# The SSM groups of a hybrid encoder layer as a table of steps: one core of a Trainium2 chip

## The chip, the core and the metric

The kernel runs on one core of one Trainium2 chip. The metric is the time of one execution in microseconds (us) as the device counts it; three runs of the kernel before were taken. The profile is one more execution, with the hardware profiler on; its rows count from the first instruction (the span).

Engines: PE is TensorE's matmul, PEld its weight load, DVE VectorE, ACT ScalarE, POOL GpSimd, SP the engine whose queue issues most DMAs. Each engine works through its own instructions in the order in which the program gives them.

## What is computed

One layer of a bidirectional encoder on 4096 tokens of width 1024, float32:

```
h = RMSNorm_pre(x)
[ssm_u | ssm_gate | pool_u | pool_gate | q | k | v | attn_gate] = h @ W_in
y_ssm  = GLU(GELU(bidirectional S5 complex-diagonal SSM(ssm_u) + D*ssm_u)) * silu(ssm_gate)
y_pool = scale * GroupLinear(centred multi-scale mean pool(pool_u) - pool_u) * silu(pool_gate)
y_attn = windowed GQA(+-128 tokens, ALiBi, sink)(q, k, v) * silu(attn_gate)
x = x + RMSNorm_post(concat(y_ssm, y_pool, y_attn) @ W_out)
```

The SSM has 16 groups of 16 channels, 64 complex states in each of two directions. A state follows h_t = lambda * h_(t-1) + B u_t with a complex lambda; y = Re(C h), summed over both directions, + D u.

## The kernel before, in words

**Stages.** TensorE multiplies float32 operands as pairs of a rounded high part and the rest (`split`, L187: ScalarE copies the high part, another engine subtracts it to get the low part, `lo_part`, one slot later), three matmuls for each product (`mm3`, L977). Pass 1 (8 blocks of 512 tokens) projects the pooling and SSM inputs, pass 2 q, k, v with the attention beside it, pass 3 the gates of SSM and attention, with the sixteen SSM groups beside it. Then comes the product with W_out, with the GLU, the pooling and the norm beside it.

**Slots.** Order is written out by hand. `Slots` (L84) holds a list of what to issue in each slot; `step()` closes one. In the projection passes a slot is 6 matmuls: a chunk (128 output channels x 512 tokens) has 24, so four slots; a block of pass 3 has six chunks, 24 slots. Chunks alternate between PSUM banks 0 and 1; a chunk's result `mm` is taken out by ScalarE in the slot after its end (`ev_g`, L1092: Silu to `gg`, stored three slots later as `sgate` or `agate`). What the program issues in a slot is added to each engine's queue; nothing else ties engines to slots, so they run ahead or behind as far as semaphores let them. `e.at` puts a function in a slot, `e.gen` a generator, whose `yield n` waits n slots. `settle` issues all that is left under a label.

**SSM groups.** `to_p3` (L1353) runs in slot 422 (block 17 of 24, its slot 14). It opens the tiles (`p3_open`, L954), where the GLU's weights are loaded and split at once (L971 to L974), and starts one generator `ssm_group` (L982) for each group, 8 slots apart (`SSM_PACE`). The sequence of eight tokens is folded into the channel dimension (128 rows = 8 tokens x 16 channels), which leaves 512 steps. With t the slot counted from a group's start, the steps are: 0 load `rec` (weights, angle tables) and `u`; 4 split `u` (low part on POOL); 6 POOL adds the angle tables to `ang`; 7 split the input weights `wb`, DVE takes the whole turns off (`kt`, `ang`, L1001, L1002); 8 ScalarE makes sine `st` and cosine `ct` (L1007 to L1009); 10, 11, 12 TensorE's products `vr`, `vi`, and the direct part into `y`; 13, 14, 15 the turn by the angle: four DVE products from PSUM, two POOL sums; split of the output weights `wc`; 16, 17 two memsets and two scans each for `gr`, `gi` (one for each direction, 64 partitions); 18 the turn back: two POOL and two DVE multiplies; 20 two POOL sums; 22, 23 splits of `hr`, `hi` (low parts on DVE); 26, 27 TensorE's last products into `y`; 28 copy, 29 store to `ybuf`. `rec` and `u` have two buffers, so the load of a group waits until the group two before has used them.

**Around the groups.** `x_load` (L288) reads a block's operands `xk` (1 MB a piece, six buffers) back for the next block on SP's queue. `load_wo` (L1071) loads W_out in halves `rawo` (three buffers) and splits each two slots later. After pass 3 the first 18 steps of the product with W_out run (L1393); at the sixth `to_c` settles what is left of the groups and starts `y_ssm` (L1178), which reads `ybuf`.

Helpers' lines stand for many operations in the profile: L162 is `tt` (tensor_tensor), L165 `stt`, L169 `ts`, L173 `copy`.

Of the kernel before, what the change touches and what calls it, by code (L numbers as in the profile page):

```python
# [10 lines left out]
F32 = mybir.dt.float32  # L11
# [5 lines left out]
P = 128  # L17
# [13 lines left out]
CH_SU, CH_SG, CH_PU, CH_PG, CH_Q, CH_K, CH_V, CH_AG = 0, 2, 4, 6, 8, 12, 13, 14  # L31

C_ID, C_D, C_E, C_CT, C_INVW, C_EDGE, C_QS = 0, 128, 512, 520, 568, 570, 602
C_NHALF, C_E1, C_HPI, C_ONE = 606, 614, 742, 743
NCST = 744
REC = 689
TWO_PI = 2.0 * math.pi
TURN = 6.283185
RND = 12582912.0


def host_constants():
    c = np.zeros((P, NCST), np.float32)
    p = np.arange(P)
    c[:, C_ID:C_ID + P] = np.eye(P)
    dist = np.abs(p[:, None] - (np.arange(3 * P)[None, :] - P))
    c[:, C_D:C_D + 3 * P] = np.where(dist <= P, -dist, -BIG)
    up = (p >= 64)[:, None]
    j = np.arange(8)[None, :]
    c[:, C_E:C_E + 8] = np.where(up, 7 - j, j)  # L50
    b = np.arange(32)[None, :]
    a = np.arange(16)[None, :]
    c[:, C_CT:C_CT + 32] = np.where(up, 31 - b, b)
    c[:, C_CT + 32:C_CT + 48] = np.where(up, 15 - a, a)
    for cc in range(2):
        w = np.where(p >= 64, 4 ** (cc + 1), 2 * 4 ** cc * 1)
        w = np.where(p >= 64, [4, 16][cc], [2, 8][cc])
        c[:, C_INVW + cc] = 1.0 / w
        h = (w // 2)[:, None]
        t = np.arange(8)[None, :]  # L60
        first = np.minimum(t + h, SEQ) - np.maximum(t - h, 0)
        tt = SEQ - 8 + t
        last = np.minimum(tt + h, SEQ) - np.maximum(tt - h, 0)
        c[:, C_EDGE + 16 * cc:C_EDGE + 16 * cc + 8] = 1.0 / first
        c[:, C_EDGE + 16 * cc + 8:C_EDGE + 16 * cc + 16] = 1.0 / last
    for cq in range(4):
# [63 lines left out]
def hybrid_kernel(ctx, tc, A, out):  # L130
# [47 lines left out]
    def bc(ap, shape):  # L178
        return ap.to_broadcast(shape)
# [774 lines left out]
    def p3_open():  # L954
        cw = ctx.enter_context(tc.tile_pool(name="cw", bufs=1))
        XTP[0] = ctx.enter_context(tc.tile_pool(name="xt3", bufs=3))
        ph = ExitStack()
        gp = ph.enter_context(tc.tile_pool(name="gp", bufs=3))
        sv = ph.enter_context(tc.tile_pool(name="sv", bufs=1))
        GP[0] = (gp, "g", "p3")  # L960
        rho = cw.tile([P, G], F32, name="rho")
        dma(out=rho, in_=rhod[:, :])
        psc = cw.tile([P, 2], F32, name="psc")
        dma(out=psc, in_=A["pool_scale"])
        gbc = cw.tile([P, DM], F32, name="gbc")
        dma(out=gbc, in_=A["post_g"])
        glb = cw.tile([P, 6], F32, name="glb")
        dma(out=glb[:, 0:4], in_=A["glu_b"])
        ts(glb[:, 4:6], glb[:, 2:4], 0.5, ALU.mult)
        gw = cw.tile([P, 2, 2, 4, P], F32R, name="gw")  # L970
        for kk in range(2):  # L971
            raw = wraw.tile([P, 4, P], F32, tag="raw", name="raw")
            dma(out=raw.rearrange("p m c -> p (m c)"), in_=A["glu_w"][:, kk])
            split(gw[:, 0, kk], gw[:, 1, kk], raw, V, 0)  # L974
        return dict(ph=ph, sv=sv, gbc=gbc, glb=glb, gw=gw, rho=rho, psc=psc)

    def mm3(o, wh, wl, r, first, last):  # L977
        T.matmul(o, lhsT=wh, rhs=r[:, 0], start=first, stop=False)
        T.matmul(o, lhsT=wh, rhs=r[:, 1], start=False, stop=False)
        T.matmul(o, lhsT=wl, rhs=r[:, 0], start=False, stop=last)  # L980

    def ssm_group(g, R):  # L982
        sv = R["sv"]
        rec = sv.tile([P, REC], F32, tag="rec", name="rec", bufs=2)
        dma(out=rec, in_=swd[g])
        u = sv.tile([P, NC], F32, tag="u", name="u", bufs=2)
        dma(out=u, in_=udram[g].rearrange("q s c -> s q c"))
        yield 4
        ur = sv.tile([P, 2, NC], F32R, tag="ur", name="ur", bufs=2)
        split(ur[:, 0], ur[:, 1], u, PL)  # L990
        yield 2

        shc = [P, 16, 32]
        ang = sv.tile(shc, F32, tag="ang", name="ang")
        tt(PL, ang, bc(rec[:, 672:688].unsqueeze(2), shc), bc(rec[:, 640:672].unsqueeze(1), shc), ALU.add)
        rho = bc(R["rho"][:, g:g + 1], [P, NC])
        yield 1
        w = sv.tile([P, 2, 3, P], F32R, tag="wb", name="wb", bufs=2)
        split(w[:, 0], w[:, 1], rec[:, 0:384].rearrange("p (m c) -> p m c", m=3), V)
        kt = sv.tile(shc, F32, tag="kt", name="kt")  # L1000
        ts(kt, ang, RND, ALU.add)  # L1001
        stt(ang, kt, RND, ang, ALU.subtract, ALU.subtract)  # L1002
        yield 1
        C_ = sv.tile([P, NC], F32, tag="ct", name="ct", bufs=2)
        S_ = sv.tile([P, NC], F32, tag="st", name="st", bufs=2)
        av = ang.rearrange("p a b -> p (a b)")
        S.activation(out=S_, in_=av, func=AF.Sin, scale=-TURN)  # L1007
        S.activation(out=C_, in_=av, func=AF.Abs)
        S.activation(out=C_, in_=C_, func=AF.Sin, scale=-TURN, bias=cst[:, C_HPI:C_HPI + 1])  # L1009
        yield 2  # L1010
        vr = bank(4, [P, NC], "vr")
        mm3(vr, w[:, 0, 0], w[:, 1, 0], ur, True, True)
        yield 1
        vi = bank(5, [P, NC], "vi")
        mm3(vi, w[:, 0, 1], w[:, 1, 1], ur, True, True)
        yield 1
        o = bank((6, 7, 2, 3)[g % 4], [P, NC], "y")
        mm3(o, w[:, 0, 2], w[:, 1, 2], ur, True, False)
        yield 1
        wr = sv.tile([P, NC], F32, tag="wr", name="wr", bufs=2)  # L1020
        wi = sv.tile([P, NC], F32, tag="wi", name="wi", bufs=2)
        t2 = sv.tile([P, NC], F32, tag="t2", name="t2")
        t3 = sv.tile([P, NC], F32, tag="t3", name="t3")
        tt(V, wr, vr, C_, ALU.mult)
        tt(V, t2, vi, S_, ALU.mult)
        yield 1
        tt(PL, wr, wr, t2, ALU.add)
        tt(V, wi, vi, C_, ALU.mult)
        tt(V, t3, vr, S_, ALU.mult)
        yield 1  # L1030
        tt(PL, wi, wi, t3, ALU.subtract)
        wc = sv.tile([P, 2, 2, P], F32R, tag="wc", name="wc", bufs=2)
        split(wc[:, 0], wc[:, 1], rec[:, 384:640].rearrange("p (m c) -> p m c", m=2), V)
        yield 1
        gr = sv.tile([P, NC], F32, tag="gr", name="gr")
        gi = sv.tile([P, NC], F32, tag="gi", name="gi")
        for gt, wt in ((gr, wr), (gi, wi)):
            V.memset(gt[0:64, 0:1], 0.0)
            V.memset(gt[64:128, NC - 1:NC], 0.0)
            V.tensor_tensor_scan(out=gt[0:64, 1:NC], data0=rho[0:64, 0:NC - 1], data1=wt[0:64, 0:NC - 1],  # L1040
                                 initial=0.0, op0=ALU.mult, op1=ALU.add)
            V.tensor_tensor_scan(out=gt[64:128, NC - 2::-1], data0=rho[64:128, 0:NC - 1],
                                 data1=wt[64:128, NC - 1:0:-1], initial=0.0, op0=ALU.mult, op1=ALU.add)
            yield 1
        tt(PL, t2, gi, S_, ALU.mult)
        tt(PL, wi, gr, S_, ALU.mult)
        tt(V, wr, gr, C_, ALU.mult)
        tt(V, t3, gi, C_, ALU.mult)
        yield 2
        tt(PL, wr, wr, t2, ALU.subtract)  # L1050
        tt(PL, wi, wi, t3, ALU.add)
        yield 2
        hr = sv.tile([P, 2, NC], F32R, tag="hr", name="hr")
        split(hr[:, 0], hr[:, 1], wr, V)
        yield 1
        hi = sv.tile([P, 2, NC], F32R, tag="hi", name="hi")
        split(hi[:, 0], hi[:, 1], wi, V)
        yield 3
        mm3(o, wc[:, 0, 0], wc[:, 1, 0], hr, False, False)
        yield 1  # L1060
        mm3(o, wc[:, 0, 1], wc[:, 1, 1], hi, False, True)
        yield 1
        y = sv.tile([P, NC], F32, tag="yg", name="yg", bufs=2)
        copy(y, o)
        yield 1
        dma(out=ybuf[g].rearrange("q s c -> s q c"), in_=y)

    WO = {}
    WO2 = [None]
# [1 line left out]
    def load_wo(slot, kk, late=False):  # L1071
        def go(hf):
            if hf == 0:
                WO[kk] = (WO2[0] if late else wpool).tile([P, 2, DM], F32R, tag="w", name="wo")
            raw = wraw.tile([P, TB], F32, tag="raw", name="rawo")
            dma(out=raw, in_=A["w_out"][kk, :, hf * TB:(hf + 1) * TB])
            e.at(e.now + 2, prep, hf, raw)

        def prep(hf, raw):
            hs = slice(hf * TB, (hf + 1) * TB)  # L1080
# [393 lines left out]
```

## Time and profile before

| | |
|---|---|
| three runs | 1682.99, 1688.07, 1686.14 us; median 1686.14 us |
| the profiled execution's own time | 1694.22 us |
| its span, instructions | 1692.4 us, 21102 |
| mean granted TensorE clock | 0.979 |
| busy | PE 93%, PEld 77%, DVE 67%, ACT 44%, POOL 37% |

A share is busy time over the span. An average over stages with different limits tells little of one stage; the rows further down are taken from the stage in which the groups run (about 935 to 1285 us). In a row of a timeline the first number is the start, the second the duration, and the brackets hold the idle time of the engine just before and what ended it. A duration runs to the end of the write; the next instruction of the same engine often starts a little before that.

### The profile page before, as it was taken

How to read it: one execution, taken by the hardware profiler on the slowest of the kernel's cores; microseconds unless marked ns; L12 is line 12 of the kernel's file. 1: busy time of each engine (PE TensorE's matmuls, PEld its weight loads, DVE VectorE, ACT ScalarE, POOL GpSimd, SP SyncE). 2: the span in 40 equal slices, each digit the busy share in tenths (PEclk: the TensorE clock that was granted, in tenths of full speed). 3: DMA queues.
4: the chain of work that ended last, by engine and by line, in shares of the span. 5: the costliest groups of instructions: out<-in, count | busy, mean ns of one | idle time of the engine just before them, and what ended most of it. 6: DMA issues, size and time to landing. Idle time of an engine off the chain costs nothing.

```text
span 1692.4 us, 21102 instructions
## 1 busy us (share of the span) xinstructions
PE 1576.4 (93%) x7364; PEld 1298.6 (77%) x7364; DVE 1128.0 (67%) x2155; ACT 744.5 (44%) x1608; POOL 629.3 (37%) x398
## 2 busy tenths in 40 slices
PE   7999799999999999999999888788779999999998
PEld 6787677788888888888888766666657788888886
DVE  5765566437777777787876477887795655555551
ACT  5423333336666666667766223323323332322231
POOL 0321212203233333332332166556662454646542
PEclk8999999999999999999999999999989999999999
DMA  6598899871211312123323544355536446454542
GB/s 225 178 300 258 252 284 294 290 265 55 68 66 63 118 64 70 63 104 100 119 89 119 196 157 155 104 167 172 178 107 211 162 150 199 157 192 161 188 144 81
DMA packets 131695, 267.60 MB, mean 158 GB/s; under 512 B 32386, under 2 KB 65922, under 8 KB 119812
## 3 DMA queue, kind: packets, MB, share of 16 engines
q1 hardware_dynamic: 126020, 251.57, 46.0%
q10 hardware_dynamic: 5568, 14.68, 2.7%
q8 instruction: 58, 0.95, 0.2%
q14 instruction: 49, 0.40, 0.1%
HBM read 173.25 MB, written 94.01 MB: 158 GB/s over the span
## 4 chain that ended last, share of the span: by engine, by line
PE 54%; DVE 14%; DMA 14%; issue 8%; POOL 6%; SPq 1%; ACT 1%; ACTq 0%; POOLq 0%; DVEq 0%
DMA xs<-in_x_dram 7%; PE mm L350 6%; PE mm L351 6%; PE mm L352 6%; PE o L1243 5%; PE o L1245 5%; PE o L1244 5%; PE po L848 5%; PE tp L858 5%; PE mm L361 3%; PE s L819 3%; PE s L818 3%; POOL wi L162 1%; DMA xt<-in_xT_dram 1%; DMA xk<-xd 1%
## 5 line engine op out<-in xcount | busy, mean ns | idle before, releaser
L350 PE MATMUL mm<-xk,w 128*128 128x512 f32 x968 | 389.9, 403 | 12.2 <-ACT gg L1103 10.4
L351 PE MATMUL mm<-xk,w 128*128 128x512 f32 x968 | 383.9, 397 | 0.0
L352 PE MATMUL mm<-xk,w 128*128 128x512 f32 x968 | 381.8, 394 | 0.5 <-DVE w L162 0.5
L162 POOL TENSOR_TENSOR ns<-ns,es 128x1536 f32<-128x1536 f32 (+1 forms) x64 | 172.5, 2696 | 409.8 <-ACT pp L173 190.2
L350 PEld LDWEIGHTS mm<-xk,w 128*128 128x128 f32 x968 | 185.1, 191 | 48.2 <-ACT gg L1103 11.2
L352 PEld LDWEIGHTS mm<-xk,w 128*128 128x128 f32 x968 | 184.8, 191 | 42.0 <-DVE w L162 1.3
L351 PEld LDWEIGHTS mm<-xk,w 128*128 128x128 f32 x968 | 185.4, 192 | 33.6 <-DVE xk L165 0.5
L1243 PE MATMUL o<-wo,yk 128*128 128x512 f32 x512 | 200.5, 392 | 3.5 <-DVE ot L165 1.8
L1245 PE MATMUL o<-wo,yk 128*128 128x512 f32 x512 | 200.2, 391 | 2.1 <-DVE yk L165 2.1
L820 DVE CUSTOM_DVE_ANT_0 ns<-s,cst,nsink 128x384 f32<-128x384 f32 (+1 forms) x256 | 145.8, 607 | 84.7 <-PE s L819 83.4
L1244 PE MATMUL o<-wo,yk 128*128 128x512 f32 x512 | 199.7, 390 | 0.0
L173 ACT ACTIVATE pp<-tp 128x512 fp32r<-128x512 f32 x188 | 112.3, 597 | 170.7 <-PE tp L858 169.7
L361 PE MATMUL mm<-xk,w 128*128 128x512 f32 x552 | 151.5, 414 | 16.5 <-ACT xk L173 10.0
L809 ACT ACTIVATE ns<-ns,nm 128x384 f32<-128x384 f32 (+1 forms) x256 | 152.4, 598 | 2.0 <-DVE nm L820 2.0
L162 DVE TENSOR_TENSOR pp<-tp,pp 128x512 fp32r<-128x512 f32 x188 | 129.2, 688 | 18.8 <-ACT pp L173 17.3
L361 PEld LDWEIGHTS mm<-xk,w 128*128 128x128 f32 x552 | 105.7, 198 | 45.4 <-ACT xk L173 14.9
L848 PE MATMUL po<-pp,vr 128*128 128x512 f32 x376 | 128.2, 422 | 0.0
L162 POOL TENSOR_TENSOR xk<-xt,xk 128x512 fp32r<-128x512 f32 x32 | 54.6, 1713 | 185.8 <-ACT xk L173 143.2
L858 PE MATMUL tp<-cst,ns 128*128 128x128 f32 x752 | 112.7, 272 | 7.3 <-DVE pp L162 7.3
L858 PEld LDWEIGHTS tp<-cst,ns 128*128 128x128 f32 x752 | 93.1, 140 | 34.4 <-issue 10.1
L1243 PEld LDWEIGHTS o<-wo,yk 128*128 128x128 f32 x512 | 96.5, 188 | 24.8 <-DVE ot L165 2.2
L1245 PEld LDWEIGHTS o<-wo,yk 128*128 128x128 f32 x512 | 96.4, 188 | 23.0 <-DVE yk L165 2.6
(308 smaller groups left out, 2710.2 us busy)
## 6 DMA issues: line engine op xcount, KB each, us to landing
xk<-xd SPq DMA_DIRECT2D x60, 1024.0 KB
xd<-xk SPq DMA_DIRECT2D x32, 1024.0 KB
xt<-in_xT_dram SPq DMA_DIRECT2D x35, 512.0 KB
xres<-in_x_dram SPq DMA_DIRECT2D x32, 512.0 KB
out_dram<-ot SPq DMA_DIRECT2D x31, 512.0 KB
xs<-in_x_dram ACTq DMA_DIRECT2D x24, 512.0 KB
raw<-in_w_in_dram SPq DMA_DIRECT2D x32, 256.0 KB
yattn<-ysb SPq DMA_DIRECT2D x32, 256.0 KB
```

Source lines behind the costliest of these rows:

```text
L162: return eng.tensor_tensor(out=out, in0=in0, in1=in1, op=op)
L350: T.matmul(o, lhsT=w[:, 0, k], rhs=xh, start=(k == 0), stop=False)
L351: T.matmul(o, lhsT=w[:, 0, k], rhs=xl, start=False, stop=False)
L352: T.matmul(o, lhsT=w[:, 1, k], rhs=xh, start=False, stop=(k == NK - 1))
L361: T.matmul(o, lhsT=w[:, i, k], rhs=XK[b, k][h], start=(n == 0), stop=(n == 3 * NK - 1))
L809: S.activation(out=ns[:, hh, :nk], in_=ns[:, hh, :nk], func=AF.Exp, scale=-1.0, bias=nm[:, hh:hh + 1], accum_out=su[:, hh:hh + 1])
L820: V.tensor_tensor_reduce(out=ns[:, hh, :nk], in0=sp_[:, :nk], in1=cst[:, C_D + c0:C_D + c0 + nk], scale=-(2.0 ** -(h + 1)), scalar=R["nsin ...
L848: T.matmul(po, lhsT=VR[:, (ta + kb) % 8, kv], rhs=pp[:, i], start=(kb == 0 and i == 0), stop=(kb == nkb - 1 and i == 1))
L858: T.transpose(tp[:, hh], ns[:, hh, kb * P:(kb + 1) * P], ident)
L1243: T.matmul(o, lhsT=y[:, 0, ts_], rhs=WO[kk][:, 0, hs], start=first, stop=False)
L1244: T.matmul(o, lhsT=y[:, 0, ts_], rhs=WO[kk][:, 1, hs], start=False, stop=False)
L1245: T.matmul(o, lhsT=y[:, 1, ts_], rhs=WO[kk][:, 0, hs], start=False, stop=last)
```

## The change

The generator becomes a function that puts 26 steps into slots in advance, as a table of (slot, function, arguments). The steps' order and places differ:

- the copies to high parts of `u` and `wb` come in slot 3, before 4 and 7; `wb`'s low part in slot 4, POOL's low part of `u` in slot 7, behind the angle sum of slot 6;
- the angles: `kt` and `ang` on DVE (L1001, L1002) are gone. ScalarE takes |a| and |a - 1/4|, then | . - 1/2| of both at once, then one Sin of both (slots 8, 9, 10); `cs` holds cosine and sine as one tile. A constant column -0.25 is added;
- `vr` and `vi` are multiplied in one slot (11), the direct part in 12;
- four DVE products and two POOL sums as before (slots 12, 13, 14), `wc`'s low part in slot 15;
- the scans write into one of two lasting tiles `gs0`, `gs1`, whose first and last columns are zeroed once in `p3_open`; the memsets in the groups are gone. Scans in slots 15 and 16;
- the turn back: one DVE multiply of 128 x 1024 by the cosine into `wt` (slot 18), one POOL multiply of 128 x 1024 by the sine, in place in `gs` (19), two POOL sums into `wt` (22, 23);
- ScalarE's high parts of the state in slots 25 and 26, DVE's low parts both in 27, the last products in 29 and 30, copy in 31, store in 33.

The GLU's weights: first load six slots after `to_p3` and split five slots later, then the second likewise. `load_wo` splits four slots after its load, not two.

```diff
@@ p3_open
-        for kk in range(2):
-            raw = wraw.tile([P, 4, P], F32, tag="raw", name="raw")
-            dma(out=raw.rearrange("p m c -> p (m c)"), in_=A["glu_w"][:, kk])
-            split(gw[:, 0, kk], gw[:, 1, kk], raw, V, 0)
+        def glu_weights():
+            for kk in range(2):
+                raw = wraw.tile([P, 4, P], F32, tag="raw", name="raw")
+                dma(out=raw.rearrange("p m c -> p (m c)"), in_=A["glu_w"][:, kk])
+                yield 5
+                split(gw[:, 0, kk], gw[:, 1, kk], raw, V)
+        e.gen(e.now + 6, glu_weights(), label="main")
+        gs = []
+        for n in range(2):
+            gt = sv.tile([P, 2, NC], F32, name=f"gs{n}")
+            V.memset(gt[0:64, :, 0:1], 0.0)
+            V.memset(gt[64:128, :, NC - 1:NC], 0.0)
+            gs.append(gt)
@@ ssm_group
...
+        def angle_abs():
+            cs = new("cs", [P, 2, NC], bufs=2)
+            av = X["ang"].rearrange("p a b -> p (a b)")
+            S.activation(out=cs[:, 0], in_=av, func=AF.Abs)
+            S.activation(out=cs[:, 1], in_=av, func=AF.Abs, bias=cst[:, C_NQ:C_NQ + 1])
+        def angle_fold():
+            S.activation(out=X["cs"], in_=X["cs"], func=AF.Abs, bias=cst[:, C_NHALF:C_NHALF + 1])
+        def angle_sin():
+            S.activation(out=X["cs"], in_=X["cs"], func=AF.Sin, scale=-TURN, bias=cst[:, C_HPI:C_HPI + 1])
...
+        def turn_re():
+            wt, t2 = new("wt", [P, 2, NC], bufs=2), new("t2", [P, 2, NC])
+            tt(V, wt[:, 0], X["vr"], X["cs"][:, 0], ALU.mult)
+            tt(V, t2[:, 0], X["vi"], X["cs"][:, 1], ALU.mult)
+        def turn_im():
+            wt, t2 = X["wt"], X["t2"]
+            tt(PL, wt[:, 0], wt[:, 0], t2[:, 0], ALU.add)
+            tt(V, wt[:, 1], X["vi"], X["cs"][:, 0], ALU.mult)
+            tt(V, t2[:, 1], X["vr"], X["cs"][:, 1], ALU.mult)
...
+        def back_cos():
+            tt(V, X["wt"], R["gs"][g % 2], bc(X["cs"][:, 0].unsqueeze(1), sh2), ALU.mult)
+        def back_sin():
+            tt(PL, R["gs"][g % 2], R["gs"][g % 2], bc(X["cs"][:, 1].unsqueeze(1), sh2), ALU.mult)
+        def back_sum(i):
+            tt(PL, X["wt"][:, i], X["wt"][:, i], R["gs"][g % 2][:, 1 - i], ALU.add if i else ALU.subtract)
...
+        for t, fn, a in ((0, load, ()), (3, inputs_hi, ()), (4, wb_lo, ()), (6, turns, ()), (7, ur_lo, ()),
+                         (8, angle_abs, ()), (9, angle_fold, ()), (10, angle_sin, ()), (11, inputs_mm, ()),
+                         (12, direct_mm, ()), (12, turn_re, ()), (13, turn_im, ()), (14, turn_sum, ()),
+                         (15, scan, (0,)), (16, scan, (1,)), (18, back_cos, ()), (19, back_sin, ()),
+                         (22, back_sum, (0,)), (23, back_sum, (1,)), (25, state_hi, (0,)), (26, state_hi, (1,)),
+                         (27, state_lo, ()), (29, state_mm, (0,)), (30, state_mm, (1,)), (31, out_copy, ()),
+                         (33, store, ())):
+            e.at(t0 + t, fn, *a, label="ssm")
@@ load_wo
-            e.at(e.now + 2, prep, hf, raw)
+            e.at(e.now + 4, prep, hf, raw)
@@ to_p3
-            e.gen(e.now + int(SSM_PACE * g), ssm_group(g, R3), label="ssm")
+            ssm_group(g, R3, e.now + int(SSM_PACE * g))
```

## Rows read from the trace of the kernel before

**Rows 1.** The page: busy tenths of TensorE and its granted clock, 40 slices.

```profile
PE   7999799999999999999999888788779999999998
...
PEclk8999999999999999999999999999989999999999
```

**Rows 2.** Windows: length, busy (count) of PE, PEld, DVE, ACT, POOL; clock, DMA, GB/s.

```profile
930.00:1285.00 355.00, 290.24 (x1181) 230.89 (x1179) 269.75 (x349) 111.21 (x204) 188.54 (x136) 0.95 0.48 158
1050.00:1090.00 40.00, 33.34 (x138) 26.64 (x137) 30.84 (x42) 11.73 (x23) 24.09 (x19) 0.96 0.45 146
1370.00:1500.00 130.00, 130.00 (x572) 107.16 (x571) 73.14 (x89) 40.55 (x76) 68.18 (x51) 1.00 0.52 169
```

**Rows 3.** Timeline of SP's queue: two loads of `rec`, one period apart.

```profile
1079.89 0.32 SPq L985 DMA_DIRECT2D rec<-swd  x1
...
1098.70 0.32 SPq L985 DMA_DIRECT2D rec<-swd  x1
```

**Rows 4.** Waits, 930 to 1290 us: total us, times, longest.

```profile
POOL t L162 <- DVE gi L1042: 124.7, 16, 8.0
...
PE y L979 <- DVE hr L162: 52.4, 16, 5.0
...
DVE kt L169 <- POOL ang L162: 32.8, 16, 6.9
DVE t L162 <- POOL wr L162: 25.6, 14, 1.8
...
PE mm L350 <- ACT gg L1103: 10.4, 2, 5.7
```

**Rows 5.** Timeline of POOL, one period.

```profile
1085.23 1.74 POOL L162 TENSOR_TENSOR t<-gi,st 128x512 f32<-128x512 f32 x1 [7.96 <-DVE gi L1042]
...
1093.40 1.28 POOL L162 TENSOR_TENSOR wr<-wr,t 128x512 f32<-128x512 f32 x1
1094.64 1.44 POOL L162 TENSOR_TENSOR wi<-wi,t 128x512 f32<-128x512 f32 x1
1104.04 1.73 POOL L162 TENSOR_TENSOR t<-gi,st 128x512 f32<-128x512 f32 x1 [7.96 <-DVE gi L1042]
```

**Rows 6.** Timeline of DVE, the same period.

```profile
1085.12 0.69 DVE L162 TENSOR_TENSOR wr<-gr,ct 128x512 f32<-128x512 f32 x1
1085.73 1.79 DVE L162 TENSOR_TENSOR t<-gi,ct 128x512 f32<-128x512 f32 x1
1087.44 0.68 DVE L162 TENSOR_TENSOR wr<-vr,ct 128x512 f32<-128x512 f32 x1
...
1093.47 1.50 DVE L169 TENSOR_SCALAR kt<-ang 128x512 f32<-128x512 f32 x1 [1.57 <-POOL ang L162]
1095.00 1.63 DVE L165 SCALAR_TENSOR_TENSOR ang<-kt,ang 128x512 f32<-128x512 f32 x1
...
1098.59 0.06 DVE L1038 MEMSET gr<- 64x1 f32 x1
...
1098.78 1.21 DVE L1040 TENSOR_TENSOR_SCAN gr<-rho,wr 64x511 f32<-64x511 f32 x1
```

**Rows 7.** Timeline of DVE, first group, POOL idle beside it.

```profile
951.64 0.43 DVE L169 TENSOR_SCALAR kt<-ang 128x512 f32<-128x512 f32 x1 [6.95 <-POOL ang L162]
952.10 0.69 DVE L165 SCALAR_TENSOR_TENSOR ang<-kt,ang 128x512 f32<-128x512 f32 x1
```

**Rows 8.** Timelines of DVE and POOL, last groups: a scan beside a sum.

```profile
1251.74 2.09 DVE L1040 TENSOR_TENSOR_SCAN gr<-rho,wr 64x511 f32<-64x511 f32 x1
...
1251.30 1.46 POOL L162 TENSOR_TENSOR wi<-wi,t 128x512 f32<-128x512 f32 x1
```

**Rows 9.** Timelines of ACT and PE at the start of the stage.

```profile
940.80 0.63 ACT L173 ACTIVATE gw<-raw 128x512 fp32r<-128x512 f32 x1 [8.45 <-DMA raw<-in_glu_w_dram]
...
940.85 0.39 PE L352 MATMUL mm<-xk,w 128*128 128x512 f32 x1
945.93 0.80 PE L350 MATMUL mm<-xk,w 128*128 128x512 f32 x1 [4.69 <-ACT gg L1103]
```

**Rows 10.** Timeline of ACT: its copy of `u` in the period of rows 3.

```profile
1103.63 0.64 ACT L173 ACTIVATE ur<-u 128x512 fp32r<-128x512 f32 x1 [4.58 <-DMA u<-udram]
```

More of the change, by code (lines that the diff above doesn't have):

```diff
@@ L33 @@
 C_ID, C_D, C_E, C_CT, C_INVW, C_EDGE, C_QS = 0, 128, 512, 520, 568, 570, 602
-C_NHALF, C_E1, C_HPI, C_ONE = 606, 614, 742, 743
-NCST = 744
+C_NHALF, C_E1, C_HPI, C_ONE, C_NQ = 606, 614, 742, 743, 744
+NCST = 745
 REC = 689
@@ L38 @@
 TURN = 6.283185
-RND = 12582912.0
 def host_constants():
@@ L72, in host_constants @@
     c[:, C_ONE] = 1.0
+    c[:, C_NQ] = -0.25
     return c
@@ L970, in p3_open @@
         gw = cw.tile([P, 2, 2, 4, P], F32R, name="gw")
-        for kk in range(2):
-            raw = wraw.tile([P, 4, P], F32, tag="raw", name="raw")
-            dma(out=raw.rearrange("p m c -> p (m c)"), in_=A["glu_w"][:, kk])
-            split(gw[:, 0, kk], gw[:, 1, kk], raw, V, 0)
-        return dict(ph=ph, sv=sv, gbc=gbc, glb=glb, gw=gw, rho=rho, psc=psc)
+        def glu_weights():
[11 more added lines that the diff above has]
+            gs.append(gt)
+        return dict(ph=ph, sv=sv, gs=gs, gbc=gbc, glb=glb, gw=gw, rho=rho, psc=psc)
     def mm3(o, wh, wl, r, first, last):
@@ L980, in mm3, with ssm_group @@
         T.matmul(o, lhsT=wl, rhs=r[:, 0], start=False, stop=last)
-    def ssm_group(g, R):
+    def ssm_group(g, R, t0):
         sv = R["sv"]
[L984 to L995, printed above, removed]
-        rho = bc(R["rho"][:, g:g + 1], [P, NC])
[L997 to L1040, printed above, removed]
-                                 initial=0.0, op0=ALU.mult, op1=ALU.add)
[L1042 to L1066, printed above, removed]
@@ new lines, in ssm_group, with new, load, inputs_hi @@
+        rho = bc(R["rho"][:, g:g + 1], [P, NC])
+        X = {}
+        def new(nm, shape, dt=F32, bufs=1):
+            X[nm] = sv.tile(shape, dt, tag=nm, name=nm, bufs=bufs)
+            return X[nm]
+        def load():
+            dma(out=new("rec", [P, REC], bufs=2), in_=swd[g])
+            dma(out=new("u", [P, NC], bufs=2), in_=udram[g].rearrange("q s c -> s q c"))
+        def inputs_hi():
+            copy(new("ur", [P, 2, NC], F32R, 2)[:, 0], X["u"])
+            copy(new("wb", [P, 2, 3, P], F32R, 2)[:, 0], X["rec"][:, 0:384].rearrange("p (m c) -> p m c", m=3))
@@ new lines, in wb_lo, with turns, ur_lo @@
+        def wb_lo():
+            w = X["wb"]
+            lo_part(w[:, 1], X["rec"][:, 0:384].rearrange("p (m c) -> p m c", m=3), w[:, 0], V)
+        def turns():
+            shc = [P, 16, 32]
+            rec = X["rec"]
+            tt(PL, new("ang", shc), bc(rec[:, 672:688].unsqueeze(2), shc), bc(rec[:, 640:672].unsqueeze(1), shc),
+               ALU.add)
+        def ur_lo():
+            lo_part(X["ur"][:, 1], X["u"], X["ur"][:, 0], PL)
+        def angle_abs():
[3 more added lines that the diff above has]
+            S.activation(out=cs[:, 1], in_=av, func=AF.Abs, bias=cst[:, C_NQ:C_NQ + 1])
@@ new lines, in angle_fold, with inputs_mm, direct_mm @@
+        def angle_fold():
+            S.activation(out=X["cs"], in_=X["cs"], func=AF.Abs, bias=cst[:, C_NHALF:C_NHALF + 1])
+        def angle_sin():
+            S.activation(out=X["cs"], in_=X["cs"], func=AF.Sin, scale=-TURN, bias=cst[:, C_HPI:C_HPI + 1])
+        def inputs_mm():
+            w, ur = X["wb"], X["ur"]
+            for i, nm in enumerate(("vr", "vi")):
+                X[nm] = bank(4 + i, [P, NC], nm)
+                mm3(X[nm], w[:, 0, i], w[:, 1, i], ur, True, True)
+        def direct_mm():
+            w = X["wb"]
+            X["o"] = bank((6, 7, 2, 3)[g % 4], [P, NC], "y")
+            mm3(X["o"], w[:, 0, 2], w[:, 1, 2], X["ur"], True, False)
@@ new lines, in turn_re, with turn_sum @@
+        def turn_re():
[7 more added lines that the diff above has]
+            tt(V, t2[:, 1], X["vr"], X["cs"][:, 1], ALU.mult)
+        def turn_sum():
+            tt(PL, X["wt"][:, 1], X["wt"][:, 1], X["t2"][:, 1], ALU.subtract)
+            wc = new("wc", [P, 2, 2, P], F32R, 2)
+            split(wc[:, 0], wc[:, 1], X["rec"][:, 384:640].rearrange("p (m c) -> p m c", m=2), V)
@@ new lines, in scan @@
+        def scan(i):
+            gs, wt = R["gs"][g % 2], X["wt"]
+            V.tensor_tensor_scan(out=gs[0:64, i, 1:NC], data0=rho[0:64, 0:NC - 1], data1=wt[0:64, i, 0:NC - 1],
+                                 initial=0.0, op0=ALU.mult, op1=ALU.add)
+            V.tensor_tensor_scan(out=gs[64:128, i, NC - 2::-1], data0=rho[64:128, 0:NC - 1],
+                                 data1=wt[64:128, i, NC - 1:0:-1], initial=0.0, op0=ALU.mult, op1=ALU.add)
+        sh2 = [P, 2, NC]
+        def back_cos():
+            tt(V, X["wt"], R["gs"][g % 2], bc(X["cs"][:, 0].unsqueeze(1), sh2), ALU.mult)
@@ new lines, in back_sin, with state_hi, state_lo @@
+        def back_sin():
+            tt(PL, R["gs"][g % 2], R["gs"][g % 2], bc(X["cs"][:, 1].unsqueeze(1), sh2), ALU.mult)
+        def back_sum(i):
+            tt(PL, X["wt"][:, i], X["wt"][:, i], R["gs"][g % 2][:, 1 - i], ALU.add if i else ALU.subtract)
+        def state_hi(i):
+            copy(new(f"h{i}", [P, 2, NC], F32R)[:, 0], X["wt"][:, i])
+        def state_lo():
+            for i in range(2):
+                h = X[f"h{i}"]
+                lo_part(h[:, 1], X["wt"][:, i], h[:, 0], V)
@@ new lines, in state_mm, with out_copy, store @@
+        def state_mm(i):
+            wc = X["wc"]
+            mm3(X["o"], wc[:, 0, i], wc[:, 1, i], X[f"h{i}"], False, i == 1)
+        def out_copy():
+            copy(new("yg", [P, NC], bufs=2), X["o"])
+        def store():
+            dma(out=ybuf[g].rearrange("q s c -> s q c"), in_=X["yg"])
+        for t, fn, a in ((0, load, ()), (3, inputs_hi, ()), (4, wb_lo, ()), (6, turns, ()), (7, ur_lo, ()),
[6 more added lines that the diff above has]
+            e.at(t0 + t, fn, *a, label="ssm")
```

## The prediction, made before the changed kernel was run

> **What bounds the kernel now.** I read the page's slices first: TensorE is nine tenths busy nearly everywhere, and the longest stretch of sevens and eights lies in slices 23 to 30, the last of them at a granted clock of 8 tenths [rows 1]. That is where the sixteen SSM groups run inside the last projection pass. The windows give its size: 355 us there hold 290 us of TensorE work at clock 0.95, and 138 matmuls per 40 us, while a clean stretch later runs 572 matmuls in 130 us, 0.227 us each [rows 2]. A group's period is the distance of two loads of `rec`, 18.81 us [rows 3]. It holds 8 slots of 6 matmuls and 15 of the group's own, 63 x 0.227 = 14.3 us, so TensorE stands still or slow for 4.5 us a group.
>
> The waits name what it waits for: 52.4 us in 16 waits for the low part of `hr` from DVE [rows 4]. A busy share cannot tell why DVE is late: it was busy 30.8 of 40 us and POOL 24.1 [rows 2], so neither looks full. But DVE waits for POOL (`ang` 32.8, `wr` 25.6) and POOL for DVE (124.7) [rows 4]: the two take turns. The timelines show how strictly. POOL works without a break from 1085.23 to 1096.08, then idles 7.96 us until the second scan is done, 1104.04 [rows 5]: 10.85 + 7.96 = 18.81, the whole period.
>
> And even inside POOL's stretch the two exclude each other. `wr<-gr,ct` takes 0.69 us; the same operation on `gi`, begun while POOL multiplies, takes 1.79 [rows 6]. `kt` and `ang` take 0.43 and 0.69 when POOL is still [rows 7], 1.50 and 1.63 beside it [rows 6]. POOL's own multiply is 1.74 there, an addition with nothing beside it 1.28 [rows 5]. A product that reads PSUM keeps its 0.68 beside POOL [rows 6]. So a DVE operation with two SBUF inputs and a POOL operation run one after the other, whatever the semaphores allow. One row shows it for a scan: 2.09 instead of 1.21 us; counted back from its end it began at 1252.62, as POOL's sum was ending [rows 6, 8]. **The stage's limit is the time in which one of the two is on, about 18.4 of the 18.81 us.** Only two pairs of memsets, 0.19 us each from the first to the scan behind them [rows 6], are outside it.
>
> **The table of steps.** It puts a group's steps into slots such that four groups interleave, loosening every chain of semaphores; it doesn't loosen the exclusion. So I count the operations of one period.
>
> Removed: `kt` and `ang` on DVE, 1.1 us together (951.64 to 952.79) [rows 7]; four memsets, 0.4 us [rows 6]. Scans, the low parts, POOL's low part of `u`, the turn sums and the angle sum stay. Two multiplies of 512 become one of 1024 on each engine: one start less each, taken as 0.15 us for both, an estimate from the 0.1 below.
>
> Handovers: counted back from its end by its 0.43, `kt` got through at 1094.54, 0.1 us before POOL's next sum begins [rows 5, 6, 7]; so a waiting partner hides about 0.1 us of POOL's start. Before, three DVE operations slip between POOL's (`t`, `kt`, `ang`). Interleaved, DVE stands ready after nearly all of POOL's seven: four more, -0.4 us.
>
> Added: I walked one period in the new order. After the second scan of group A come `back_cos` (DVE), `back_sin` (POOL), the two low parts of the state of the group before, the first two turn products of group B, then POOL's sum of these. POOL's next instruction after `back_sin` is that sum, so it stands still while DVE makes the two products from PSUM: 2 x 0.68 = 1.3 us [rows 6] with nobody in SBUF. Behind it the two alternate to the period's end: sum, scans, back sum, turn sum, angles, low part. The bounds: 0 if POOL is ahead in another order, 2.6 if the second pair is exposed too; I take 1.3, for the order is fixed on both queues.
>
> Period: 18.81 - 1.1 - 0.4 - 0.15 - 0.4 + 1.3 = 18.06, say 18.0 us; bounds 16.7 (products covered) and 18.8. The first group is paced by TensorE in both kernels, so 14 periods: 14 x 0.8 = **11 us** (bounds 0 and 29).
>
> The Trainium skill (SBUF — State Buffer, Who interferes with whom) states that a DVE instruction with two SBUF inputs and a GpSimd instruction that reads SBUF block each other for the whole instruction, but its list of operations that do so has tensor_tensor, tensor_scalar and copies and no scan. By the list alone the four scans would be free of it, which is rival 1 below; by the rule of two inputs they are not, and the one row of a scan beside POOL is with the rule.
>
> **Angles on ScalarE.** ScalarE gets two Abs of 512, one Abs and one Sin of 1024 for three operations of 512: about 1.3 us more a group, doubling 0.6 us pieces. It is busy 11.7 of 40 us [rows 2], and the table gives each a slot of its own: nothing. Without that cover it would delay evictions of `mm`, whose price is the last point below.
>
> **Lasting state tiles.** They take the memsets away (counted). `back_sin` writes in place what `back_cos` reads, so POOL waits for one DVE multiply, 1.2 us; the exclusion orders them so anyway: nothing.
>
> **GLU weights late.** Now ScalarE waits 8.45 us for the raw weights at the stage's start, the eviction behind it is late, and TensorE stands 4.69 us, its next matmul at 0.80 instead of 0.39 [rows 9]. Loaded at slot 6 and split five slots later, the weights are there. On SP their two loads move behind `rec` and `u` of group 0 and one `xk` load, which makes `u` earlier and delays the last `xk` by one 256 KB transfer. TensorE can use the 4.69 only as far as the chain of the first groups starts earlier with it; the loads of group 1 stand in SP's queue behind `xk` loads that wait for TensorE, so nearly all: **5 us** (bounds 0, and 7: an estimate, 4.69 and six matmuls slower by that 0.4).
>
> **Later tail, later split of W_out.** The last product of a group comes in slot 30 instead of 27, so 4 instead of 7 slots (1.36 us each, 6 x 0.227) remain to TensorE after the last group: up to 4 us less, if the exclusion sets the end; the store comes 4 slots later, 5.5 us more if the GLU's chain waits for it. The store then still has seven slots before that load. I take -2. The split of `rawo` two slots later holds one of three buffers 2.7 us longer; SP waits with the next load, and `sgate`/`agate` stores and `ya` loads queue behind it. They aren't awaited at once; what it covers is ScalarE's wait for raw data, which stands before evictions (the second of the two waits for `gg`, 5.7 us [rows 4]). Nothing, bounds -5 and +3.
>
> On SP, `rec` still waits for the low part of `wc`, now in slot 15 instead of 16, and the copies come in slot 3 instead of 4: the same distance. `u` reaches ScalarE 4.9 us after `rec` is issued (1098.70 to 1103.63) [rows 3, 10]; the walk leaves twice that.
>
> **Sum.** 11 + 5 + 2 = 18 us off the profiled execution's 1694.2 (span 1692.4). That execution is 8 us above the median of the runs, 1686.1, which I take it off: **1668 us**.
>
> **Rivals.**
> 1. *TensorE sets the pace.* If scans go beside POOL freely, the excluded time falls to 18.06 - 1.3 - 4 x 1.21 = 11.9 us, below 14.3, and TensorE runs through: 14 x 4.5 + 7 = 70 us, **1616**. For it: every semaphore chain has several slots of slack in the table. Against: the 2.09 us [rows 8]. Chance 0.09.
> 2. *The exclusion costs more than now.* POOL's queue stands at a sum while DVE makes all four products, 2.6 us, and no handover is hidden. Place: between `back_sin` and the scans. Period 18.06 + 1.3 + 0.4 = 19.8, 14 x 0.95 = 13 us more, less 5 for the GLU: **1694**. It decides for slower once the period is over 19.3 (7 us of other gains over 14 periods above 18.81). For it: DVE and POOL queues are in order and each now serves four groups. Against: the second products need nothing from POOL and run while it sums. Chance 0.11.
> 3. *Nothing changes hands.* The period stays, the exposed products eating what was removed, and the GLU's stall only turns into a wait for the first groups: 0 to 5 us, **1684**. Chance 0.10.
>
> **How the numbers follow.** My forecast has 0.70. Its bounds added (29 + 7 + 4 = 40 us) give 1646 at best; its other end is rival 3's. Range 1645 to 1686: rivals 1 and 2 stay out, 0.20. About 0.3%, 5 us, is what a measurement of this kernel can tell from no change. Faster 0.70 + 0.09 = 0.79, same 0.10, slower 0.11.
>
> **What would show it.** Right: a period near 18.0 between `rec` loads; DVE and POOL rows still stretched beside each other, and scans now too, near 2.3 us; TensorE still waiting some 3.6 us a group, at another product (the first of `vr`, for POOL's low part of `u`, or the state's low part); no TensorE wait for `gg` at the stage's start. Wrong: scans of 1.21 beside a busy POOL and a period of 14.3 (rival 1); a period above 19 with gaps in which both stand still (rival 2).

## The result and the profile after

The changed kernel took 1664.61 us (median of 4 runs, 1663.26 to 1665.48) beside 1686.03 us for the kernel before: ratio 0.9878, 95% interval 0.986 to 0.9896. The forecast was 1668, "faster" with 0.79. In a later series the same pair gave 0.9901 (0.9883 to 0.9918), so the gain is 17 to 21 us. The direction, the size and the stage are as forecast; several of the terms behind the size are not, as the experiments show.

The first fence is SP's queue in the changed kernel, the loads of `rec` that gave the period in [rows 3].

```profile
1075.04 0.32 SPq L1006 DMA_DIRECT2D rec<-swd  x1
...
1092.74 0.32 SPq L1006 DMA_DIRECT2D rec<-swd  x1
```

The period is 17.70 us, down from 18.81; over the last twelve groups it is (1181.33 - 968.76) / 12 = 17.71. TensorE would need 14.3. The waits of the stage (930 to 1290 us) show where it stands now, beside [rows 4]:

```profile
POOL gs L162 <- DVE wt L162: 41.7, 15, 6.0
POOL wt L162 <- DVE t L162: 36.4, 15, 4.8
...
PE vr L991 <- POOL ur L162: 30.2, 14, 3.6
...
PE y L991 <- DVE h L162: 9.6, 1, 9.6
```

TensorE's 52.4 us for the state's low part have become 30.2 us for POOL's low part of `u`, as the forecast's last paragraph named it, and one wait of 9.6 us near the end. DVE no longer waits for POOL through a semaphore in any row above 4 us, and yet the two have not come apart. A row of windows shows what happened, the changed kernel's 40 us beside the same 40 us in [rows 2] (columns as there):

```profile
1050.00:1090.00 40.00, 35.53 (x148) 28.38 (x147) 39.53 (x31) 15.96 (x27) 30.79 (x17) 0.96 0.44 140
```

DVE's busy time rose from 30.8 to 39.5 of 40 us, though `kt`, `ang` and four memsets a group were taken from it. It is not doing more; its operations last longer. One period of DVE (compare [rows 6]):

```profile
1073.88 1.10 DVE L162 TENSOR_TENSOR wc<-rec,wc 128x256 fp32r<-128x256 f32 x1
1074.90 2.30 DVE L1069 TENSOR_TENSOR_SCAN gs<-rho,wt 64x511 f32<-64x511 f32 x1
1077.21 2.13 DVE L1071 TENSOR_TENSOR_SCAN gs<-rho,wt 64x511 f32<-64x511 f32 x1
1079.37 1.22 DVE L162 TENSOR_TENSOR wt<-gs,cs 128x1024 f32<-128x1024 f32 x1
1080.52 3.48 DVE L162 TENSOR_TENSOR h<-wt,h 128x512 fp32r<-128x512 f32 x2
1084.13 0.69 DVE L162 TENSOR_TENSOR wt<-vr,cs 128x512 f32<-128x512 f32 x1
1084.74 0.68 DVE L162 TENSOR_TENSOR t<-vi,cs 128x512 f32<-128x512 f32 x1
1085.34 0.55 DVE L162 TENSOR_TENSOR wb<-rec,wb 128x384 fp32r<-128x384 f32 x1
1085.80 0.68 DVE L162 TENSOR_TENSOR wt<-vi,cs 128x512 f32<-128x512 f32 x1
1086.40 0.68 DVE L162 TENSOR_TENSOR t<-vr,cs 128x512 f32<-128x512 f32 x1
```

and of POOL (compare [rows 5]):

```profile
1074.66 1.46 POOL L162 TENSOR_TENSOR wt<-wt,gs 128x512 f32<-128x512 f32 x1
1076.07 2.19 POOL L162 TENSOR_TENSOR ur<-u,ur 128x512 fp32r<-128x512 f32 x1
1080.67 2.77 POOL L162 TENSOR_TENSOR gs<-gs,cs 128x1024 f32<-128x1024 f32 x1 [2.42 <-DVE wt L162]
1085.56 1.48 POOL L162 TENSOR_TENSOR wt<-wt,t 128x512 f32<-128x512 f32 x1 [2.11 <-DVE t L162]
```

A scan that took 1.21 us takes 2.13 to 2.30 beside a busy POOL (2.3 was forecast), and POOL's low part of `u` 2.19 where an addition alone took 1.28 [rows 5]. Each waits inside its own instruction for the other, and the profile counts that as busy. The products from PSUM keep their 0.69 and 0.68. The gap that the forecast added is there too: POOL stands 2.11 us before its sum. In the first 0.56 of them DVE still makes the second low part of the state (until 1084.00), then the two products that the sum needs (until 1085.42); for these 1.4 us neither engine holds the other up.

Where the time went, by the marks of the two profiled executions (the issue of `rho` when the stage opens; `rec` of group 3; `rec` of group 15; the first matmul with W_out):

| stretch, us | before | after |
|---|---|---|
| start of the stage to group 3 | 50.98 | 43.70 |
| group 3 to group 15 (12 periods) | 225.50 | 212.57 |
| group 15 to the first matmul with W_out | 71.16 | 70.05 |
| the whole stage | 347.64 | 326.32 |

21.3 us were gained in the stage. From there to the end the changed kernel is 1.8 us longer in this execution; in its second profile (experiment 5) it is 0.8 us shorter than the kernel before, so that stretch tells nothing. The profiled execution of the kernel before had also spent 9.9 us more ahead of the stage, in code that the change does not touch; that is why the two spans differ by 29 us and the medians by 21.

### The profile page after: what moved, and what is told of

The parts are those of the page before. It is cut to its first block, busy times and chain, and to the rows that moved or that the text cites. A ratio compares the mean times of both kernels' runs of the same rounds, so it can differ in the third digit from the quotient of the medians.

```text
span 1663.0 us, 20965 instructions
## 1 busy us (share of the span) xinstructions
PE 1574.8 (95%) x7364; PEld 1296.1 (78%) x7364; DVE 1152.4 (69%) x2047; ACT 766.5 (46%) x1624; POOL 665.0 (40%) x382
## 4 chain that ended last, share of the span: by engine, by line
PE 57%; DVE 22%; DMA 11%; issue 4%; POOL 4%; ACT 2%; SPq 1%; ACTq 0%; DVEq 0%; POOLq 0%
PE mm L350 7%; PE mm L351 7%; PE mm L352 7%; PE po L848 5%; DMA xs<-in_x_dram 5%; PE tp L858 5%; PE o L1289 5%; PE o L1287 5%; PE o L1288 5%; DVE gs L1069 4%; DVE gs L1071 4%; PE mm L361 4%; DVE h L162 3%; PE s L819 3%; PE s L818 3%
## 5 line engine op out<-in xcount | busy, mean ns | idle before, releaser
L162 DVE TENSOR_TENSOR pp<-tp,pp 128x512 fp32r<-128x512 f32 x188 | 129.1, 687 | 18.8 <-ACT pp L173 17.4
```

Source lines behind the costliest of these rows:

```text
L162: return eng.tensor_tensor(out=out, in0=in0, in1=in1, op=op)
```

## The experiments

All ratios are to the kernel before on the same chip.

**1. The scans' decay factor in PSUM.** This is the direct test of the exclusion: where one operand of the scans lies is changed, and to make room for it the direct part gets three PSUM banks instead of four.

```diff
-        rho = cw.tile([P, G], F32, name="rho")
-        dma(out=rho, in_=rhod[:, :])
+        rho_s = cw.tile([P, G], F32, name="rho")
+        dma(out=rho_s, in_=rhod[:, :])
+        rho = bank(3, [P, G], "rhop")
+        V.tensor_copy(out=rho, in_=rho_s)
...
-            X["o"] = bank((6, 7, 2, 3)[g % 4], [P, NC], "y")
+            X["o"] = bank((6, 7, 2)[g % 3], [P, NC], "y")
```

> The changed kernel with the scans' decay factor read from a PSUM bank instead of SBUF, so that a scan has one SBUF input; the direct part uses three banks instead of four. Theory (a DVE operation with two SBUF inputs and a POOL operation exclude each other): the four scans, 1.21 us each, fall out of the excluded time, 17.7 - 4.8 = 12.9 us, below TensorE's 14.3; the period between loads of rec falls from 17.70 to between 14.3 and 15.0, scans take 1.2 to 1.4 us beside a busy POOL, and the time falls by 14 x 3 = 40 us or more below the changed kernel's 1664.6, to 1605 to 1625. Rival (scans are long in the new trace for another reason, such as the write of a strided tile or a wait that the profile counts as busy): scans stay near 2.2 us, the period stays at 17.7 and the time at 1664.

Measured: 1613.81 us, ratio 0.9589 (0.9573 to 0.9605). The scans and the POOL operations beside them in this kernel (timelines of DVE, then POOL):

```profile
1061.60 1.21 DVE L1071 TENSOR_TENSOR_SCAN gs<-rhop,wt 64x511 f32<-64x511 f32 x1
1062.82 1.23 DVE L1073 TENSOR_TENSOR_SCAN gs<-rhop,wt 64x511 f32<-64x511 f32 x1
...
1061.52 1.31 POOL L162 TENSOR_TENSOR wt<-wt,gs 128x512 f32<-128x512 f32 x1
1062.77 1.31 POOL L162 TENSOR_TENSOR wt<-wt,t 128x512 f32<-128x512 f32 x1
```

The two run side by side at the speed that each has alone. SP's loads and one window:

```profile
1051.43 0.32 SPq L1008 DMA_DIRECT2D rec<-swd  x1
1065.44 0.32 SPq L1008 DMA_DIRECT2D rec<-swd  x1
```

```profile
1050.00:1090.00 40.00, 40.00 (x177) 32.85 (x176) 38.70 (x37) 20.90 (x34) 28.10 (x20) 1.00 0.62 199
```

The period is 14.0 us, 171.1 / 12 = 14.26 on average: TensorE's own 14.3. It is busy for all 40 us, at clock 1.00 instead of 0.96, with 177 matmuls for 138 in [rows 2]. The exclusion is shown, and shown to be what limited the stage. (The fourth bank isn't the reason: the same edit in the kernel before, experiment 8, changes nothing.) This version beats both kernels, the changed one by about 50 us.

**2. Filling POOL's gap.** The angle sum stands in slot 4 instead of 6.

```diff
-(4, wb_lo, ()), (6, turns, ()), (7, ur_lo, ()),
+(4, wb_lo, ()), (4, turns, ()), (7, ur_lo, ()),
```

> The changed kernel with POOL's angle sum of a group in slot 4 instead of 6, so that it stands in POOL's queue behind the back multiply and before the turn sum. Theory: POOL does it (about 1.0 us) while DVE makes the two products from PSUM, in which nobody is in SBUF; the period falls by 0.9 to 1.1 us, from 17.70 to 16.7, 14 x 1.0 = 14 us off 1664.6: 1651. Rival (the gap on POOL costs nothing, for DVE is the full engine): period 17.7, time within 3 us of 1664.6.

Measured: 1655.43 us, ratio 0.9838 (0.9822 to 0.9854); the period is 17.03, 0.7 less. The gap costs what the theory says in kind, two thirds of it in size. POOL's timeline shows the sum in its new place:

```profile
1060.87 1.49 POOL L162 TENSOR_TENSOR ang<-rec 128x512 f32<-128x512 f32 x1
1063.02 1.47 POOL L162 TENSOR_TENSOR wt<-wt,t 128x512 f32<-128x512 f32 x1 [0.66 <-DVE t L162]
```

The sum takes 1.49 us, where it took 1.04 in the kernel before (at 1092.39): it waits first for DVE's second low part of the state. 0.66 us of the gap are left. The missing third is taken up again below.

**3. DVE instead of POOL for the low part of `u`.**

```diff
-            lo_part(X["ur"][:, 1], X["u"], X["ur"][:, 0], PL)
+            lo_part(X["ur"][:, 1], X["u"], X["ur"][:, 0], V)
```

> The changed kernel with the low part of u made by DVE instead of POOL. DVE shows as busy nearly without a break in the stage, POOL has gaps of 4.5 us a period. Theory (exclusion): the operation holds SBUF for 0.55 us on DVE instead of 1.15 on POOL, so the period falls by about 0.6 us, to 17.1, and the time by 8 us to 1656. Rival (DVE's own work is the limit): DVE gets 0.6 us more, the period rises to 18.3, the time to 1673.

Measured: 1662.74 us, ratio 0.988 (0.9864 to 0.9897), period 17.40. More work for the engine that shows as 99% busy made the period 0.3 us shorter, not 0.6 longer: the rival falls. Only half of the expected gain came. By the marks the stage is 3.8 us shorter than the changed kernel's (322.49 beside 326.32); the two times, each known to about 3 us, can't tell that from nothing. POOL now idles 4.05 us in a period, while DVE's second pair of scans and its multiply by the cosine run alone:

```profile
1078.13 2.71 POOL L162 TENSOR_TENSOR gs<-gs,cs 128x1024 f32<-128x1024 f32 x1 [4.05 <-DVE wt L162]
```

TensorE's waits for `xk` rose from 1.5 to 7.7 us in this profile. Why these rose wasn't followed.

**4, 5. GLU weights early again.** The old lines of the weights' load in the changed kernel, timed twice, the second time beside the changed kernel itself on one chip.

> The changed kernel with the GLU weights loaded and split at the start of the stage, as before the change. Theory: TensorE waits 4 to 5 us for the eviction gg at the stage's start again, the period stays at 17.7, and the time rises by 5 us to 1670. Rival (TensorE's start is hidden, since the exclusion sets the stage's end): time within 2 us of 1664.6 although the wait is back.

Measured first: 1668.17 us, ratio 0.991 (0.9892 to 0.9927), which beside 0.9878 would be the 5 us of the forecast. But the profile gave 328.26 us for the stage beside 326.32, only 2 us. So once more, with the changed kernel beside it:

> The changed kernel itself, as the reference on this chip for the next three. Both theories of each: ratio to the kernel before 0.988, period 17.7.

> The changed kernel with the GLU weights at the start of the stage, once more, beside the changed kernel on the same chip, since the trace shows 2 us for it in the stage and the first timing 5. Forecast's term: 5 us slower than the changed kernel. Rival (the stage's end is set by the exclusion, so only part of TensorE's wait counts): 1 to 3 us slower.

Measured: changed kernel 1668.23 us, ratio 0.9901 (0.9883 to 0.9918); with early weights 1667.41 us, ratio 0.9898 (0.9885 to 0.9912). The times show no difference, though TensorE's wait is back (timeline of PE, early weights):

```profile
934.00 0.50 PE L350 MATMUL mm<-xk,w 128*128 128x512 f32 x1 [3.96 <-ACT gg L1143]
```

The 5 us of the first reading weren't confirmed. The marks of both pairs agree on a smaller effect: with early weights the stretch up to the load of group 3 is 2 us longer (45.64 beside 43.70, and 46.01 beside 43.97), and the twelve periods behind it are the same. The late weights also moved ScalarE's wait: with them it stands at the stage's start for `u` instead (changed kernel):

```profile
937.20 0.63 ACT L173 ACTIVATE ur<-u 128x512 fp32r<-128x512 f32 x1 [10.68 <-DMA u<-udram]
```

**6. The angles alone, in the old order.** Kernel before, with `kt` and `ang` gone and four ScalarE operations as in the change.

```diff
...
-        kt = sv.tile(shc, F32, tag="kt", name="kt")
-        ts(kt, ang, RND, ALU.add)
-        stt(ang, kt, RND, ang, ALU.subtract, ALU.subtract)
...
-        S.activation(out=S_, in_=av, func=AF.Sin, scale=-TURN)
-        S.activation(out=C_, in_=av, func=AF.Abs)
-        S.activation(out=C_, in_=C_, func=AF.Sin, scale=-TURN, bias=cst[:, C_HPI:C_HPI + 1])
+        S.activation(out=C_, in_=av, func=AF.Abs)
+        S.activation(out=S_, in_=av, func=AF.Abs, bias=cst[:, C_NQ:C_NQ + 1])
+        S.activation(out=cs, in_=cs, func=AF.Abs, bias=cst[:, C_NHALF:C_NHALF + 1])
+        S.activation(out=cs, in_=cs, func=AF.Sin, scale=-TURN, bias=cst[:, C_HPI:C_HPI + 1])
```

> The kernel before with one part of the change alone: the angles folded on ScalarE, kt and ang on DVE gone; order and slots as before. Theory (a period is the time in which DVE, with two SBUF inputs, or POOL is on): kt and ang hold SBUF for 0.35 and 0.6 us, so the period falls from 18.8 by 0.9 to 1.0 us to 17.8 and the time by 14 us, to 1670. Rival (the gain is the interleaving): period within 0.3 us of 18.8, time within 5 us of the kernel before.

Measured: 1663.41 us, ratio 0.9882 (0.9867 to 0.9896), period 17.55. One part of the change gives all of its gain, with a shorter period than the whole. The loads that give the period, and TensorE's waits in this kernel (925 to 1290 us):

```profile
1061.53 0.33 SPq L986 DMA_DIRECT2D rec<-swd  x1
1079.08 0.32 SPq L986 DMA_DIRECT2D rec<-swd  x1
```

```profile
PE mm L351 <- ACT gg L1102: 22.6, 10, 4.7
PE mm L362 <- ACT gg L1102: 7.8, 4, 2.2
PE y L980 <- DVE hr L163: 5.1, 2, 3.5
```

The wait for the low part of the state, 52.4 us in the kernel before [rows 4], has become a wait for the eviction `gg`. In the period after the one shown ScalarE's copy of `hr` waits 3.83 us for POOL's sum, the eviction stands behind it, and TensorE waits 2.15 us for that. So in that period POOL still holds TensorE up, by another way.

**7. The table without the angles.** The changed kernel with `kt` and `ang` on DVE (slot 8), and Sin, Abs, Sin of 512 on ScalarE (slots 9, 10).

```diff
...
         def angle_abs():
+            kt, ang = new("kt", [P, 16, 32]), X["ang"]
+            ts(kt, ang, RND, ALU.add)
+            stt(ang, kt, RND, ang, ALU.subtract, ALU.subtract)
...
```

> The changed kernel with the angles as before the change: kt and ang on DVE (slot 8), Sin, Abs and Sin of 512 on ScalarE. What is left of the change is the table, the lasting tiles and the late weights. Theory: the period rises by what the two hold, 0.35 + 0.6, to 18.6 to 18.9, about that of the kernel before: the interleaving by itself gains nothing, and the time is 1675 to 1681, ratio 0.994 to 0.999, with what the late GLU weights give. Rival (the interleaving carries part of the gain): period below 18.3, ratio below 0.992.

Measured: 1680.99 us, ratio 0.9981 (0.997 to 0.9991), period 18.77. On DVE the two stand with nothing beside them, 1.07 us from the first's start to the next operation's (helper lines are one further here and in 6):

```profile
1087.08 0.43 DVE L170 TENSOR_SCALAR kt<-ang 128x512 f32<-128x512 f32 x1
1087.54 0.69 DVE L166 SCALAR_TENSOR_TENSOR ang<-kt,ang 128x512 f32<-128x512 f32 x1
1088.15 1.22 DVE L163 TENSOR_TENSOR wt<-gs,cs 128x1024 f32<-128x1024 f32 x1
```

18.77 - 17.70 = 1.07: the price is that (1.05 by the means of twelve periods). Table, lasting tiles and late weights together are worth 0.2%, 3 us.

**8. The decay factor in PSUM, in the old order.** Edit as in 1, in the kernel before.

> The kernel before with the scans' decay factor read from PSUM, and nothing else but three banks for the direct part. Theory: in the old order POOL stands still while the scans run, for it waits for them; so freeing the scans of the exclusion gives nothing there: scans stay at 1.22, the period at 18.8 and the time within 3 us of the kernel before. That would make the table of steps worth little by itself and much together with the PSUM factor. Rival (a scan with one SBUF input is itself what helps, or it frees POOL also in the old order): period below 18.0, time below 1672.

Measured: 1683.65 us, ratio 1.0004 (0.9993 to 1.0016), period 18.80. As the theory had it, POOL waits for the scans anyway (timelines of DVE, then POOL):

```profile
1090.26 1.22 DVE L1044 TENSOR_TENSOR_SCAN gi<-rhop,wi 64x511 f32<-64x511 f32 x1
...
1091.62 1.74 POOL L162 TENSOR_TENSOR t<-gi,st 128x512 f32<-128x512 f32 x1 [7.96 <-DVE gi L1044]
```

**9. Both, in the old order.** Edits of 6 and 8 together.

> The kernel before, in its old order, with the angles on ScalarE and the decay factor in PSUM. Theory: in the old order POOL waits for the scans anyway, so nothing beyond the angles' own gain: period 17.55, ratio 0.988. Rival (the two changes alone, without the table, bring the stage to TensorE's pace): period 14 to 15, ratio 0.96.

Measured: 1662.52 us, ratio 0.9875 (0.986 to 0.989), period 17.6: the angles' gain and no more. So the same edit of one operand is worth nothing in the old order and 50 us in the new one. The table and the operand without the angles were not run.

**10. Memsets back** in front of each pair of scans of the changed kernel.

```diff
         def scan(i):
             gs, wt = R["gs"][g % 2], X["wt"]
+            V.memset(gs[0:64, i, 0:1], 0.0)
+            V.memset(gs[64:128, i, NC - 1:NC], 0.0)
```

> The changed kernel with the two memsets in front of each pair of scans again, so that a period has four more DVE instructions of 0.06 us. Theory: they cost 0.4 us in a period only where nobody else is in SBUF in the meantime; in the new order POOL's operation runs beside them, so I expect 0 to 0.2 us a period, 0 to 3 us in all. The forecast had counted 0.4 us a period for their removal: then the time rises by 5 to 6 us, to 1669.

Measured: 1664.77 us, ratio 0.9893 (0.9874 to 0.9913), period 17.70 as without them. DVE's timeline: the scan behind the memsets takes 2.10 instead of 2.30, so their 0.2 us went into the time that it waits for POOL anyway.

```profile
1061.87 0.06 DVE L1069 MEMSET gs<- 64x1 f32 x1
1061.99 0.06 DVE L1070 MEMSET gs<- 64x1 f32 x1
1062.06 2.10 DVE L1071 TENSOR_TENSOR_SCAN gs<-rho,wt 64x511 f32<-64x511 f32 x1
```

**11. The split of W_out two slots after its load** in the changed kernel.

```diff
-            e.at(e.now + 4, prep, hf, raw)
+            e.at(e.now + 2, prep, hf, raw)
```

> The changed kernel with the split of W_out two slots after its load, as before the change. Theory: off the path, within 2 us of the changed kernel. Rival: ScalarE waits longer for raw data, the eviction gg comes late once more and TensorE waits 3 to 6 us at the end of the stage: time up by that much.

Measured: 1664.16 us, ratio 0.9886 (0.9871 to 0.9901): no difference in the time. In its profile the first matmul with W_out comes 72.70 us after the last load of `rec`, not 70.05, and the rest is shorter by as much and a little more.

## Why the prediction was right, and which terms were not

**The limit was read rightly.** The stage is bounded by the time in which DVE, with two SBUF inputs, or POOL is on. Experiment 1 shows it by taking scans out, 3 by moving work to the fuller engine, 7 by putting work back. Rival 1 (TensorE's pace) stood on scans that pass POOL freely; they don't, unless an operand lies elsewhere, and then its period of 14.3 comes out. The Trainium skill's rule (SBUF — State Buffer, Who interferes with whom) that a DVE instruction with two SBUF inputs contends with a GpSimd instruction that reads SBUF holds here for scans too: 2.13 to 2.30 us with two, 1.21 with one. The forecast's own wording of the rule is too narrow for one of its rows: `kt` reads a single SBUF tile and was stretched as well, 1.50 us beside POOL [rows 6] for 0.43 [rows 7]. It was counted among the excluded operations all the same, so the sum didn't suffer.

**The table's term.** Forecast 18.06 us a period, measured 17.71. By parts:
- `kt` and `ang`: 1.1 forecast; 1.07 in the new order (7), 1.25 in the old (6). This is where the gain comes from.
- Memsets: 0.4 forecast, 0 measured in the new order (10). The step took them from the old order, where nothing ran beside them, and subtracted them in the new one, where a wait absorbs them.
- Exposed products: +1.3 forecast; the rows above give 1.4 us in which neither engine holds the other up, and putting the angle sum there gave 0.7 (2).
- Handovers: mis-sized. The forecast took 0.1 us as hidden at each of four more. The scans shown above end 2.14 us apart (1077.20 and 1079.34) with POOL's low part of `u` between them; one after the other the two would take 1.21 + 1.28 = 2.49, so a turn of both engines hides about 0.3. POOL's rows before [rows 5] had it already: the sum beside `kt` took 1.44 instead of 1.28, 0.16 more for a `kt` of 0.43; the forecast looked only at the start of that sum. With 0.3 four times, and the multiplies' 0.15 as forecast, 18.81 - 1.07 - 0.15 - 1.2 + 1.4 = 17.8. This is an estimate from single rows, and no run varied the handovers alone. But experiments 2 and 3 each take one POOL operation out from between two DVE operations, and each fell about 0.3 us short of what was expected.
- All of the table without the angles: -0.4 - 0.15 - 0.4 + 1.3 = +0.35 a period forecast, 18.77 against 18.81 measured (7). With the angles already gone it is +0.15 (17.70 against 17.55). So what interleaving hides it loses in the gap, as forecast; by the estimate above it hid more than assumed.

**The GLU's term failed.** 5 us forecast; the times of the pair run together show none, within 4 us by the two intervals, and the marks 2 us (5). The failing step is that "nearly all" of TensorE's wait could be used, for the loads of group 1 stood behind loads that wait for TensorE. They do start earlier, 6.66 us after group 0's instead of 12.33. But ScalarE then stands 10.68 us for `u` of group 0 in the same place. That the rest is lost because the exclusion sets the stage's end is argued; no run shows it by itself. Rival 3's half sentence, that the stall only turns into a wait for the first groups, came nearer.

**The tail's term** was near in size, -2 forecast and -1.1 by the marks; with the late split, five profiles of the new order at a period of 17.7 give 69.1 to 70.2 us for the stretch, two of the old order at 18.8 give 71.2 and 71.9. But it holds a wait of 9.57 us that the forecast didn't have, beside the pooling's POOL and DVE work. TensorE's timeline there:

```profile
1229.69 0.80 PE L991 MATMUL y<-h,wc 128*128 128x512 f32 x1 [9.57 <-DVE h L162]
```

No run took that wait away by itself, so what it costs is open.

**The total.** 11 + 5 + 2 was forecast. By the marks the stage gained 12.9 in the twelve periods, 7.3 in the first groups, where the rest of the 14 periods and the late weights count, and 1.1 at the end. The total was closer than its terms: the memsets and the GLU were taken too high and the handovers too low, and that these nearly cancel is luck.

**Rival 2** didn't come: the second pair of products runs under POOL's sum, which was the argument against it. **W_out's split** cost nothing, as costed (11). That the **angles on ScalarE** cost nothing in the new order fits the waits, where TensorE stands for `gg` only 2.0 and 2.6 us, but no run of the new order separates it from what it frees on DVE.

## What to carry to other kernels

Before interleaving two engines' steps, ask whether the two can run at once: look for an operation that lasts longer beside the other engine than alone, and add up the time in which either is on. If that sum is the period, reordering alone gains little (here 3 us of 1684), taking an operation off both engines gains up to its length (here 1.07 us a period for `kt` and `ang`), and moving one operand to PSUM may free an operation altogether. Order and operand may then have to be changed together: here the operand alone gave 0, and with the table and the angles 70 us.

## What the runs showed that was not expected

Reading the scans' decay factor from PSUM cost the scan nothing (1.21 and 1.23 us, as in SBUF) and moved the whole kernel by 3%. And busy time misled: DVE's rose to 39.5 of 40 us with fewer operations, because a wait for the other engine lies inside the instruction; giving it more work (3) made the period 0.3 us shorter.
